# A two-block fp32 network on one core: the rows of silu(c) made by TensorE, the first loads in one queue and another order, and the input-norm generator of layer 1 queued later

## The chip, the cores and the metric

The kernel runs on one core of one Trainium2 chip. The metric is the device time of one execution in microseconds. It is given as the median of three runs. The engines are named as the profile names them: PE is TensorE (its weight loads are PEld), DVE is VectorE, ACT is ScalarE, POOL is GpSimd, and SP is SyncE, which here only issues DMAs.

## The reference

Two blocks follow each other. The first has two layers over 1024 tokens of x and 256 tokens of context, 1024 wide. The second has one layer and a gated feed-forward part. What the change touches lies in the first block:

```python
def hybrid_layer(x, xc, c_act, cc_act, w_mod, b_mod, ...):
    shift, scale, gate = jnp.split(c_act @ w_mod + b_mod, 3, axis=-1)
    h = x * (1 + scale[:, None]) + shift[:, None]
    rk, rv, nk, nv, rq, rg, nq, ng, ch, cb, ccg, cz = split_cols(h @ w_in, PROJ_SPLITS)
    ...
    y = jnp.concatenate([y_conv, y_ret, y_na], axis=-1) @ w_out
    x_new = layer_norm(DEEPNORM_ALPHA * x + gate[:, None] * y, ln_g, ln_b)

def first_block(...):
    c_act = jax.nn.silu(c)
    cc_act = jax.nn.silu(c_ctx)
    for l in range(DEPTH):
        x, xc = hybrid_layer(x, xc, c_act, cc_act, ...)
```

`y_ret` is a retention over 6 heads, forward and backward, and `y_na` is an attention over a window of 8 x 16 neighbours and the context, with 6 heads.

## The kernel before

Every fp32 product is split: an operand is a high part that TensorE takes at its fast fp32 form and a low part, and three matmuls (high x high, high x low, low x high) are summed. So a weight block is loaded raw (`wr`), ACT makes its high part (`wh`) and POOL its low part (`wl = wr - wh`); three raw buffers and three pairs of high and low rotate. The split of hidden states is the same work on ACT and DVE (`xh`, `xl` for x, `ch`, `cl` for the context).

The order of the work is set by a planner, the class Mixer. It keeps a modelled time `vt` that advances with each TensorE product. Generators for side work (retention pairs, attention pairs, modulation blocks and so on) are queued with `mix.add`. Each main product earns credit (`ratio` times its own time), and while there is credit the first generator that is due is stepped, so that side work stands between main products. `R_RET` is that ratio in the retention part. A generator that yields a number is due again that many nanoseconds later. `mix.drain()` steps all that is left, moving `vt` on to each generator's due time. TensorE's queue has the order in which products are emitted. On the other engines instructions are ordered by the modelled start time that they had (plus `late`, 5000 ns for the generators with X_MOD); on the chip each queue then runs strictly in order, SP's queue of DMA issues too.

The start. `setup` loads c as a column (`cvec`) and, by two broadcast DMAs, as rows (`crow`, each 128 x 1024). `hidden0_load(k)` loads for one of 8 blocks of 128 features a column block of the scale weights transposed (`wmT`), a block of the shift weights (`wm`) and x and context transposed (`xr`, `xc`). `hidden0` makes block k of the modulated hidden state: `mod_block` reduces wmT times each row of `crow` on DVE (into `mjk`), which gives the scale; eight small products `cact, wm` on TensorE give the shift; ACT applies both; `split` makes the high and low parts. `ready_k` runs `STEPS` blocks ahead of the first main product that needs block k. The first main products (`wh`, `wl` against `xh`, `xl`, `ch`, `cl`) are the values of the retention heads.

The end of a layer. The attention pairs n0 to n2 run beside main products. Then come gate blocks, `mix.drain()`, and the output projection, which reads `yr` (the layer's y back from DRAM, split to `yhl`) against `w_out`, one weight block for twelve matmuls. Its result is normalised. `x1_gen` belongs to layer 1: layer 0 left its norm without gain and bias in DRAM (`xn`), and this generator loads each of 8 token tiles, multiplies by the gain and adds the bias on POOL (tiles `x`, 128 x 1024, against `lnbc`), and stores them as `x1`, which the end of layer 1 reads. It is a loop of these lines:

```python
for t in range(8):
    x = self.S("x1")
    self.nc.sync.dma_start(out=x, in_=self.xn[sl])
    yield
    self.tt(x, x, gb[0], ALU.mult, self.nc.gpsimd)
    self.tt(x, x, gb[1], ALU.add, self.nc.gpsimd)
    self.nc.sync.dma_start(out=self.x1[0][sl], in_=x)
    self.free(x)
    yield 6000
```

In profiles, line L344 is the helper of every matmul, L349 that of every transpose, and L251 records each operation of the other engines.

Of the kernel before, what the change touches and what calls it, by code (L numbers as in the profile page):

```python
# [12 lines left out]
AF = mybir.ActivationFunctionType  # L13
ALU = mybir.AluOpType
AX = mybir.AxisListType

NX = 1024
NC = 256
NT = NX + NC
# [7 lines left out]
class Mixer:  # L27
# [92 lines left out]
    late = 0.0  # L120
# [362 lines left out]
class Layers(Base):  # L483
    X_RET = (1500, 1500)
    AHEAD = 3
    STEPS = 2
# [3 lines left out]
    def setup(self):  # L490
        nc, io = self.nc, self.io
        self.cvec = self.const("cvec", [128, 16])
        nc.sync.dma_start(out=self.cvec, in_=io["c_cols"])
        self.bmod = self.const("bmod", [128, 48])
        nc.sync.dma_start(out=self.bmod, in_=io["b_mod"])
        self.crow = [self.S("crow") for _ in range(2)]
        for j in range(2):
            nc.scalar.dma_start(out=self.crow[j], in_=io["c_rows"][j:j + 1, :].to_broadcast([128, 1024]))
        self.mjk = self.S("mjk")
        self.h0 = {}  # L500
        for k in range(self.AHEAD):
            self.hidden0_load(k)
        self.ident = self.const("ident", [128, 128])
        nc.sync.dma_start(out=self.ident, in_=io["c_ident"])
        self.ones = self.const("ones", [128, 128])
        nc.vector.memset(self.ones, 1.0)
        self.mhalf = self.const("mhalf", [128, 16])
        nc.gpsimd.memset(self.mhalf, -0.5)
        self.lncol = self.const("lncol", [128, 32])
        nc.sync.dma_start(out=self.lncol, in_=io["ln_col"])  # L510
        self.convw = self.const("convw", [128, 16])
        nc.sync.dma_start(out=self.convw, in_=io["conv"])
        self.iota = self.const("iota", [128, 4])
        nc.sync.dma_start(out=self.iota, in_=io["c_iota"])

        self.cact = self.const("cact", [128, 8, 2])
        t = self.small("cs", [128, 16])
        self.act(t, self.cvec, AF.Tanh, scale=0.5)
        self.stt(t, t, 1.0, self.cvec, ALU.add, ALU.mult)
        for j in range(2):  # L520
            self.ts(self.cact[:, :, j], t[:, 8 * j:8 * j + 8], 0.5, None, ALU.mult)
        for c in self.crow:
            t = self.S("crt")
            self.act(t, c, AF.Tanh, scale=0.5)
            self.stt(c, t, 1.0, c, ALU.add, ALU.mult)
            self.free(t)

        self.ts(self.bmod[:, 8:16], self.bmod[:, 8:16], 1.0, None, ALU.add)

        self.mod = [self.const(f"mod{l}", [128, 3, 8, 2]) for l in range(2)]  # L530

    def mod_block(self, l, b, w, nctx=2):

        acc = self.small("macc", [128, 2])
# [3 lines left out]
        part, kk = divmod(b, 8)  # L538
        self.ts(self.mod[l][:, part, kk, 0:nctx], acc[:, 0:nctx], 0.5, self.bmod[:, 24 * l + b:24 * l + b + 1], ALU.mult, ALU.add)
# [17 lines left out]
    def hidden0_load(self, k):  # L557
        if k < 8:
            io, nc = self.io, self.nc
# [3 lines left out]
            nc.scalar.dma_start(out=t, in_=io["xT"][k * 128:(k + 1) * 128, 0:NX])  # L563
            nc.scalar.dma_start(out=c, in_=io["xT"][k * 128:(k + 1) * 128, NX:NT])
# [35 lines left out]
    def ret_consts(self, l):  # L600
# [3 lines left out]
        nc.sync.dma_start(out=E, in_=io["c_E"])  # L604
        nc.sync.dma_start(out=x, in_=io["ret_decay"][l:l + 1, :].to_broadcast([128, 12]))
# [478 lines left out]
    R_RET = 10.0  # L1084
# [16 lines left out]
    def layer(self, l, hT, need_ctx, ready=None, ready_k=None):  # L1101
# [24 lines left out]
        for s in self.ORDER1[l].split():  # L1126
# [11 lines left out]
            else:  # L1138
                if p == 0 and l == 1:
                    mix.add(self.x1_gen(), True, peak=3, late=self.X_MOD)  # L1140
# [474 lines left out]
    def block1(self, stop=None):  # L1615
        nc, io, mix = self.nc, self.io, self.mix
        self.done_o, self.ready = set(), set()
        self.w_init()
        for l in range(2):
            self.layer_weights(l)  # L1620
# [963 lines left out]
def host_layout(inputs):  # L2584
# [15 lines left out]
    a["c_rows"] = np.concatenate([f("c"), f("c_ctx")[None]], 0)  # L2600
# [109 lines left out]
```

## Time and profile before

| | before |
|---|---|
| runs | 2966.71, 2963.77, 2957.46 us |
| median | 2963.77 us |
| profiled execution | 2959.18 us |
| its span | 2957.4 us |
| mean granted TensorE clock | 0.957 |
| busy: PE, DVE, ACT, POOL | 92%, 67%, 40%, 33% |

The profiled execution is one of the kernel, taken apart from the three runs; its span goes from the first to the last instruction, and the rest of its time lies around that. Busy shares are of the span. A granted clock of 1.00 is the full rate.

### The profile page before, as it was taken

What the parts mean: (1) busy time and instruction counts of PE and PEld (TensorE: products, weight loads), DVE (VectorE), ACT (ScalarE), POOL (GpSimd) and SP (SyncE); (2) the same over time, 40 slices, a digit from 0 to 9 for tenths busy, and PEclk for the clock granted to TensorE, in tenths of its full rate; (3) what the DMA queues carried; (4) which work ended last, traced back from release to release, by engine and by line L of the source; (5) the groups of instructions that cost most, each with busy time, mean ns of one, the idle gap of its engine ahead of it and who ended that gap; (6) DMA issues with size and microseconds to landing.
All of it is one profiled execution on the core that took longest, in us unless ns stands there. A gap on an engine that the chain in (4) does not pass through costs nothing. (4 is left out here: it accounts for less than half of the span.)

```text
span 2957.4 us, 41337 instructions
## 1 busy us (share of the span) xinstructions
PE 2722.3 (92%) x14572; PEld 2342.2 (79%) x14572; DVE 1985.9 (67%) x4011; ACT 1190.1 (40%) x2715; POOL 971.4 (33%) x836
## 2 busy tenths in 40 slices
PE   6989999999989989979999977899998999999998
PEld 6977888898788878768787766787876788887886
DVE  6866675774642557667554697868844588786687
ACT  5212254563332225445443332456653333333443
POOL 4443512213433441451563332111135244443001
PEclk9988999999999999989999979999999999999999
DMA  7533302216333221433543543222343222223874
GB/s 254 180 103 124 93 32 78 82 65 202 127 108 100 65 70 34 154 119 131 169 135 108 170 139 123 99 72 85 109 158 125 96 107 107 107 96 122 305 252 168
DMA packets 173071, 367.87 MB, mean 124 GB/s; under 512 B 30048, under 2 KB 57984, under 8 KB 172864
## 3 DMA queue, kind: packets, MB, share of 16 engines
q1 hardware_dynamic: 160064, 343.07, 34.3%
q10 hardware_dynamic: 10016, 13.12, 1.8%
q0 software_dynamic: 2784, 9.05, 1.0%
q8 instruction: 115, 1.88, 0.3%
q14 instruction: 92, 0.75, 0.1%
HBM read 279.35 MB, written 79.51 MB: 121 GB/s over the span
## 5 line engine op out<-in xcount | busy, mean ns | idle before, releaser
L251 POOL TENSOR_TENSOR wl<-wr,wh 128x512 fp32r<-128x512 f32 (+2 forms) x344 | 452.1, 1318 | 1151.0 <-ACT wh L251 1046.9
L344 PE MATMUL pb<-xl,wh 128*128 128x512 f32 x1456 | 580.2, 399 | 0.0
L344 PE MATMUL pb<-xh,wl 128*128 128x512 f32 x1456 | 579.5, 398 | 0.6 <-POOL wl L251 0.6
L344 PE MATMUL pb<-xh,wh 128*128 128x512 f32 x1456 | 579.1, 398 | 0.0
L251 ACT ACTIVATE wh<-wr 128x512 fp32r<-128x512 f32 (+2 forms) x344 | 202.7, 591 | 401.7 <-PE pb L344 314.4
L344 PEld LDWEIGHTS pb<-xh,wl 128*128 128x128 f32 x1456 | 277.6, 191 | 56.5 <-POOL wl L251 1.0
L344 PEld LDWEIGHTS pb<-xl,wh 128*128 128x128 f32 x1456 | 277.8, 191 | 54.1 <-issue 0.2
L344 PEld LDWEIGHTS pb<-xh,wh 128*128 128x128 f32 x1456 | 277.7, 191 | 53.0 <-issue 0.3
L344 PE MATMUL pb<-wh,yhl 128*128 128x512 f32 x832 | 264.0, 396 | 7.0 <-DVE xl L251 4.4
L344 PE MATMUL pb<-T,wh 128*128 128x512 f32 x640 | 196.9, 389 | 0.0
L344 PEld LDWEIGHTS pb<-wh,yhl 128*128 128x128 f32 x832 | 158.4, 191 | 41.3 <-issue 6.0
L251 POOL TENSOR_TENSOR wl<-ws,wh 128x512 fp32r<-128x512 f32 x100 | 135.0, 1350 | 155.4 <-ACT wh L251 154.0
L344 PE MATMUL pb<-wl,yhl 128*128 128x512 f32 x416 | 164.8, 396 | 5.1 <-POOL wl L251 5.1
L344 PE MATMUL pb<-whi,yhl 128*128 128x512 f32 x528 | 164.0, 392 | 4.5 <-DVE yhl L251 4.5
L251 ACT ACTIVATE pt<-pb 128x512 fp32r<-128x512 f32 (+3 forms) x230 | 114.0, 528 | 132.4 <-PE pb L349 115.5
L251 DVE TENSOR_TENSOR pt<-pb,pt 128x512 fp32r<-128x512 f32 (+3 forms) x230 | 130.0, 595 | 51.5 <-ACT pt L251 50.3
L344 PEld LDWEIGHTS pb<-T,wh 128*128 128x128 f32 x640 | 120.1, 188 | 25.0
L251 DVE TENSOR_TENSOR yhl<-yr,yhl 128x512 fp32r<-128x512 f32 (+2 forms) x133 | 97.6, 760 | 61.4 <-ACT yhl L251 52.4
L251 ACT ACTIVATE wh<-ws 128x512 fp32r<-128x512 f32 x100 | 63.2, 632 | 172.7 <-PE pb L344 172.7
L344 PE MATMUL pb<-wl,xh 128*128 128x384 f32 (+1 forms) x384 | 125.9, 328 | 5.9 <-POOL wl L251 5.9
L344 PE MATMUL pb<-wh,xl 128*128 128x384 f32 (+1 forms) x384 | 126.0, 328 | 3.4 <-ACT wh L251 1.3
L344 PE MATMUL pb<-wh,xh 128*128 128x384 f32 (+1 forms) x384 | 125.4, 327 | 0.0
(434 smaller groups left out, 6009.5 us busy)
## 6 DMA issues: line engine op xcount, KB each, us to landing
wr<-in_w_in_dram SPq DMA_DIRECT2D x152, 256.0 KB, 2.7
ws<-in_w_down_dram SPq DMA_DIRECT2D x110, 256.0 KB, 5.6
wr<-in_w_out_dram SPq DMA_DIRECT2D x96, 256.0 KB, 2.9
yr<-ffn SPq DMA_DIRECT2D x33, 512.0 KB, 5.8
wm<-in_w_modT_dram SPq DMA_DIRECT2D x32, 512.0 KB, 4.8
wr<-in_w_v_dram SPq DMA_DIRECT2D x64, 192.0 KB, 2.4
ws<-in_w_gate_dram SPq DMA_DIRECT2D x22, 512.0 KB, 5.3
ws<-in_w_up_dram SPq DMA_DIRECT2D x22, 512.0 KB, 6.1
```

What stands on the lines that cost most here:

```text
L251: return fn(*a, **kw)
L344: self.mix.product(c / 2.4, out, (lhsT, rhs), lambda: self.nc.tensor.matmul(out, lhsT, rhs, start=start, stop=stop))
```

## The change

Setup makes the rows of silu(c) from the column form: for each of the two vectors DVE writes eight 128 x 128 blocks, the identity times one column of silu(c) (`crt`), TensorE multiplies them with a matrix of ones in two products of 512 columns, and ACT copies the results to `crow`. The two broadcast loads, two tanh and two products on whole rows go; the factor 0.5 is now in `cact`, so `mod_block` drops it. `ident` and `bmod` are loaded in ACT's queue. The transposed x and context move from ACT's queue to SP's, behind the weights of their block, and the first three value weights stand between the loads of block 0 and block 1. `STEPS` is 1. The load of layer 0's retention decay gets a copy in front that reads the last modulation scale, so that it can't be issued before that is there. `R_RET` is 2. `x1_gen` is no longer started at gate block 0 of layer 1 but queued at gate block 2.

```diff
@@ setup
         nc.sync.dma_start(out=self.cvec, in_=io["c_cols"])
+        self.ident = self.const("ident", [128, 128])
+        nc.scalar.dma_start(out=self.ident, in_=io["c_ident"])
         self.bmod = self.const("bmod", [128, 48])
-        nc.sync.dma_start(out=self.bmod, in_=io["b_mod"])
+        nc.scalar.dma_start(out=self.bmod, in_=io["b_mod"])
+        self.h0 = {}
+        self.hidden0_load(0)
+        self.w_init()
+        self.layer_weights(0)
+        self.w_load(self.NRAW)
+        self.hidden0_load(1)
...
+        self.act(t, self.cvec, AF.Tanh, scale=0.5)
+        self.stt(t, t, 1.0, self.cvec, ALU.add, ALU.mult)
+        for j in range(2):
+            self.ts(self.cact[:, :, j], t[:, 8 * j:8 * j + 8], 0.5, None, ALU.mult)
         self.crow = [self.S("crow") for _ in range(2)]
         for j in range(2):
-            nc.scalar.dma_start(out=self.crow[j], in_=io["c_rows"][j:j + 1, :].to_broadcast([128, 1024]))
+            t = self.S("crt", (128, 8, 128))
+            for k in range(8):
+                self.ts(t[:, k], self.ident, self.cact[:, k, j:j + 1], None, ALU.mult)
+            for i in range(2):
+                ps = self.bank()
+                self.mm(ps, self.ones, t[:, 4 * i:4 * i + 4])
+                self.act(self.crow[j][:, 512 * i:512 * i + 512], ps)
+            self.free(t)
...
-        for k in range(self.AHEAD):
+        for k in range(2, self.AHEAD):
             self.hidden0_load(k)
...
-        for c in self.crow:
-            t = self.S("crt")
-            self.act(t, c, AF.Tanh, scale=0.5)
-            self.stt(c, t, 1.0, c, ALU.add, ALU.mult)
-            self.free(t)
@@ class Layers
-    STEPS = 2
+    STEPS = 1
...
-    R_RET = 10.0
+    R_RET = 2.0
@@ mod_block
-        self.ts(self.mod[l][:, part, kk, 0:nctx], acc[:, 0:nctx], 0.5, self.bmod[:, 24 * l + b:24 * l + b + 1], ALU.mult, ALU.add)
+        self.ts(self.mod[l][:, part, kk, 0:nctx], acc[:, 0:nctx], self.bmod[:, 24 * l + b:24 * l + b + 1], None, ALU.add)
@@ hidden0_load
-            nc.scalar.dma_start(out=t, in_=io["xT"][k * 128:(k + 1) * 128, 0:NX])
-            nc.scalar.dma_start(out=c, in_=io["xT"][k * 128:(k + 1) * 128, NX:NT])
+            nc.sync.dma_start(out=c, in_=io["xT"][k * 128:(k + 1) * 128, NX:NT])
+            nc.sync.dma_start(out=t, in_=io["xT"][k * 128:(k + 1) * 128, 0:NX])
@@ ret_consts
+        if l == 0:
+            nc.vector.tensor_copy(x[:, 0:1], self.mod[0][:, 1, 7, 0:1])
         nc.sync.dma_start(out=x, in_=io["ret_decay"][l:l + 1, :].to_broadcast([128, 12]))
@@ the pairs of layer l
-                if p == 0 and l == 1:
-                    mix.add(self.x1_gen(), True, peak=3, late=self.X_MOD)
+                if p == 2 and l == 1:
+                    mix.add(self.x1_gen(), peak=3, late=self.X_MOD)
@@ block1
-        self.w_init()
-        for l in range(2):
-            self.layer_weights(l)
+        self.layer_weights(1)
```

What the planner makes of it is seen in three queues. First POOL in layer 1's output projection. Names `wl` are low parts of weights, and `x` the tiles of x1_gen. Before (`wl_13735` is the first weight of the projection, and all of x1_gen stands earlier):

```order
L251 TENSOR_TENSOR wl_13729<-wr_13361,wh_13728 128x512
L251 TENSOR_TENSOR wl_13735<-wr_13367,wh_13734 128x512
L251 TENSOR_TENSOR wl_13893<-wr_13726,wh_13892 128x512
L251 TENSOR_TENSOR wl_13917<-wr_13732,wh_13916 128x512
L251 TENSOR_TENSOR wl_13939<-wr_13890,wh_13938 128x512
L251 TENSOR_TENSOR wl_13961<-wr_13914,wh_13960 128x512
```

Now (`wl_13728` is the first weight; each tile x has two rows, of which the first is shown, except for the last):

```order
L251 TENSOR_TENSOR wl_13728<-wr_13346,wh_13727 128x512
...
L251 TENSOR_TENSOR x_2763_13652<-x_2763_13652,lnbc_13575 128x1024
...
L251 TENSOR_TENSOR wl_13916<-wr_13719,wh_13915 128x512
L251 TENSOR_TENSOR wl_13940<-wr_13725,wh_13939 128x512
L251 TENSOR_TENSOR x_2794_13763<-x_2794_13763,lnbc_13575 128x1024
...
L251 TENSOR_TENSOR x_2797_13801<-x_2797_13801,lnbc_13575 128x1024
...
L251 TENSOR_TENSOR x_2800_13816<-x_2800_13816,lnbc_13576 128x1024
L251 TENSOR_TENSOR wl_13962<-wr_13913,wh_13961 128x512
L251 TENSOR_TENSOR wl_13984<-wr_13937,wh_13983 128x512
```

Two tiles (four rows) now stand between the first and the second weight of the projection, and six tiles (twelve rows) between the third and the fourth.

Second, SP's queue at the same place, where `x_0_56_192` is the store of a tile x and `xn_194` its source. Now:

```order
L251 DMA x_0_56_192<-x_2797_13801 128x1024
L251 DMA x_2799_13811<-xn_194 128x1024
L251 DMA x_2800_13816<-xn_194 128x1024
L251 DMA x_0_56_192<-x_2798_13806 128x1024
...
L251 DMA x_0_56_192<-x_2799_13811 128x1024
L251 DMA yr_13899<-yT_5_51_187 128x512
L251 DMA x_0_56_192<-x_2800_13816 128x1024
L251 DMA yr_13931<-yT_6_52_188 128x512
L251 DMA wr_13937<-in_w_out_dram 128x512
L251 DMA yr_13955<-yT_7_53_189 128x512
```

The raw load of the fifth weight (`wr_13937`, which `wl_13984` above reads) and the last two `yr` now stand behind the store of the last tile x; before, no transfer of x1_gen stood among them.

Third, DVE at the start. Before:

```order
L251 TENSOR_SCALAR cact<-cs_120 128x8 x2
L251 SCALAR_TENSOR_TENSOR crow_78<-crt_125,crow_78 128x1024
L251 SCALAR_TENSOR_TENSOR crow_79<-crt_128,crow_79 128x1024
L251 ISA mjk_82,macc_192<-wmT_83,crow_78 128x1024
...
L251 ISA mjk_82,macc_256<-wmT_99,crow_78 128x1024
...
L251 TENSOR_TENSOR cl_187<-xc_86,ch_186 128x256
```

Now:

```order
L251 TENSOR_SCALAR cact<-cs_105 128x8 x2
L251 TENSOR_SCALAR crt_112<-ident,cact 128x128 x8
L251 TENSOR_SCALAR crt_127<-ident,cact 128x128 x8
L251 ISA mjk_143,macc_220<-wmT_80,crow_110 128x1024
...
L251 ISA mjk_143,macc_309<-wmT_144,crow_110 128x1024
...
L251 TENSOR_TENSOR cl_215<-xc_83,ch_214 128x256
```

The sixteen blocks take the place of the two products on rows, and block 0's low part `cl` stands, as before, behind the reduction of block 2's `wmT`.

## Rows read from the trace of the kernel before

**Rows 1.** The page of the profile: busy time and share of each engine.
```profile
PE 2722.3 (92%) x14572; PEld 2342.2 (79%) x14572; DVE 1985.9 (67%) x4011; ACT 1190.1 (40%) x2715; POOL 971.4 (33%) x836
```

**Rows 2.** Stretches: start:end, length, then busy us per engine, granted clock, DMA share, GB/s.
```profile
0.00:50.00 50.00, 29.05 (x153) 28.09 (x154) 30.77 (x51) 22.64 (x42) 15.73 (x15) 1.00 0.91 319
...
1235.00:1298.00 63.00, 38.77 (x214) 34.61 (x213) 45.94 (x104) 27.15 (x79) 35.68 (x23) 0.78 0.36 124
...
1400.00:1435.00 35.00, 35.00 (x156) 28.99 (x155) 12.80 (x16) 12.91 (x22) 17.39 (x13) 1.00 0.58 181
```

**Rows 3.** Timeline of TensorE, start: start us, us, instruction, [idle before, what ended it].
```profile
10.91 1.41 PE L344 MATMUL pb<-cact,wm 128*128 128x2 f32 x6 [10.91 <-DMA wm<-in_w_mod_dram]
...
30.68 0.69 PE L344 MATMUL pb<-wh,cl 128*128 128x384 f32 x1 [9.22 <-DVE cl L251]
...
56.64 0.66 PE L344 MATMUL pb<-wh,cl 128*128 128x384 f32 x1 [4.25 <-DVE mod L251]
...
61.30 1.84 PE L344 MATMUL pb<-cact,wm 128*128 128x2 f32 x16
```

**Rows 4.** Timeline of VectorE, start of the kernel.
```profile
17.61 2.36 DVE L251 SCALAR_TENSOR_TENSOR crow<-crt,crow 128x1024 f32<-128x1024 f32 x2 [11.54 <-ACT crt L251]
19.89 1.22 DVE L251 CUSTOM_DVE_ANT_0 mjk<-wmT,crow 128x1024 f32<-128x1024 f32 x1
...
56.08 0.41 DVE L251 TENSOR_TENSOR cl<-xc,ch 128x256 fp32r<-128x256 f32 x1
```

**Rows 5.** DMA view of 44 to 46 us, SP's queue: packets, MB, share of 16 engines.
```profile
q1 hardware_dynamic: 225, 0.79, 101.3%
```

**Rows 6.** Groups of TensorE by form: busy us, mean ns; a product with ones.
```profile
L344 PE MATMUL pb<-dg,ones 128*128 128x128 f32 x48 | 6.5, 298 | 1.0 <-DVE dg L251 1.0
```

**Rows 7.** Waits of TensorE, 235 to 275 us: total us, times, longest us.
```profile
PE pb L344 <- DVE sd L251: 1.2, 1, 1.2
```

**Rows 8.** Waits of TensorE, 1236 to 1298 us.
```profile
PE pb L349 <- DVE sl L251: 19.5, 5, 5.9
PE pb L344 <- DVE pt L251: 4.5, 2, 2.3
```

**Rows 9.** Waits of TensorE, 540 to 575 us (the same stretch of layer 0).
```profile
PE pb L349 <- DVE sl L251: 3.2, 3, 1.9
PE pb L344 <- DVE pt L251: 2.0, 2, 1.7
```

**Rows 10.** Timeline of VectorE and of POOL from 1258 us.
```profile
1258.34 0.34 DVE L251 TENSOR_SCALAR sl<-sl,rsm 128x256 f32<-128x256 f32 x1
1258.60 2.42 DVE L251 TENSOR_SCALAR sc<-sc,rsm 128x256 f32<-128x256 f32 x1
1260.95 2.56 DVE L251 TENSOR_SCALAR sl<-sl,rsm 128x384 f32<-128x384 f32 x1
...
1258.35 4.95 POOL L251 TENSOR_TENSOR x<-x,lnbc 128x1024 f32<-128x1024 f32 x2 [4.61 <-DMA yT<-go]
```

**Rows 11.** Instructions on the tiles x, 1210 to 1320 us: min/median/max ns, first and last start.
```profile
L251 POOL TENSOR_TENSOR x<-x,lnbc x16: 2338/2384/2532, 1217.4 to 1313.8; 128x1024 f32<-128x1024 f32 x16
```

**Rows 12.** Timeline of POOL, from 1397 us: the low parts of weights.
```profile
1397.93 1.29 POOL L251 TENSOR_TENSOR wl<-wr,wh 128x512 fp32r<-128x512 f32 x1 [18.79 <-ACT wh L251]
1400.64 1.49 POOL L251 TENSOR_TENSOR wl<-wr,wh 128x512 fp32r<-128x512 f32 x1 [1.42 <-ACT wh L251]
1403.59 1.44 POOL L251 TENSOR_TENSOR wl<-wr,wh 128x512 fp32r<-128x512 f32 x1 [1.46 <-ACT wh L251]
```

**Rows 13.** Timeline of TensorE, layer 1's output projection.
```profile
1399.90 0.39 PE L344 MATMUL pb<-wh,yhl 128*128 128x512 f32 x1
...
1408.29 0.39 PE L344 MATMUL pb<-wl,yhl 128*128 128x512 f32 x1
```

**Rows 14.** DMA issues of the page: count, KB each, median us from issue to landing.
```profile
wr<-in_w_out_dram SPq DMA_DIRECT2D x96, 256.0 KB, 2.9
```

More of the change, by code (lines that the diff above doesn't have):

```diff
@@ L493, in setup @@
         nc.sync.dma_start(out=self.cvec, in_=io["c_cols"])
+        self.ident = self.const("ident", [128, 128])
+        nc.scalar.dma_start(out=self.ident, in_=io["c_ident"])
         self.bmod = self.const("bmod", [128, 48])
-        nc.sync.dma_start(out=self.bmod, in_=io["b_mod"])
+        nc.scalar.dma_start(out=self.bmod, in_=io["b_mod"])
[5 more added lines that the diff above has]
+        self.hidden0_load(1)
+        self.ones = self.const("ones", [128, 128])
+        nc.vector.memset(self.ones, 1.0)
+        self.cact = self.const("cact", [128, 8, 2])
+        t = self.small("cs", [128, 16])
+        self.act(t, self.cvec, AF.Tanh, scale=0.5)
+        self.stt(t, t, 1.0, self.cvec, ALU.add, ALU.mult)
+        for j in range(2):
+            self.ts(self.cact[:, :, j], t[:, 8 * j:8 * j + 8], 0.5, None, ALU.mult)
         self.crow = [self.S("crow") for _ in range(2)]
         for j in range(2):
-            nc.scalar.dma_start(out=self.crow[j], in_=io["c_rows"][j:j + 1, :].to_broadcast([128, 1024]))
+            t = self.S("crt", (128, 8, 128))
[6 more added lines that the diff above has]
+            self.free(t)
+        self.ts(self.bmod[:, 8:16], self.bmod[:, 8:16], 1.0, None, ALU.add)
         self.mjk = self.S("mjk")
-        self.h0 = {}
-        for k in range(self.AHEAD):
+        for k in range(2, self.AHEAD):
             self.hidden0_load(k)
[L503 to L506, printed above, removed]
         self.mhalf = self.const("mhalf", [128, 16])
@@ L514, in setup @@
         nc.sync.dma_start(out=self.iota, in_=io["c_iota"])
[L516 to L521, printed above, removed]
-        for c in self.crow:
-            t = self.S("crt")
-            self.act(t, c, AF.Tanh, scale=0.5)
-            self.stt(c, t, 1.0, c, ALU.add, ALU.mult)
-            self.free(t)
-        self.ts(self.bmod[:, 8:16], self.bmod[:, 8:16], 1.0, None, ALU.add)
         self.mod = [self.const(f"mod{l}", [128, 3, 8, 2]) for l in range(2)]
@@ L2599, in host_layout @@
     a["w_modT"] = np.ascontiguousarray(wm.transpose(0, 2, 1)).reshape(2, 24, 128, 1024)
-    a["c_rows"] = np.concatenate([f("c"), f("c_ctx")[None]], 0)
     w = f("w_in")
```

## The prediction

> **What bounds the kernel now.** I read the busy shares first: TensorE works 92% of the span [rows 1], and nothing in the change removes work from it, so a gain can only come out of TensorE's idle time or its slow stretches, and a loss can only be new idle time. Then I read stretches of 50 us, and looked for those with idle time next to the places that the diff touches. Three matter [rows 2]: the first 50 us (29.05 us busy), the drain of layer 1's attention at 1235 to 1298 us (38.77 us busy of 63, granted clock 0.78), and the output projection of layer 1 from 1400 us, where TensorE has no idle time at all at a clock of 1.00. The timeline says what ends each idle time.
>
> **The start.** TensorE's first product waits 10.91 us for `wm`, the first main product stands at 30.68 after a wait of 9.22 us for `cl`, and the first main product of block 4 at 56.64 after 4.25 us [rows 3]. Behind the second wait stands DVE: it could not begin the reductions (`mjk`) before `crow` was made, at 17.61 to 19.89 us [rows 4], and from there to 61 us it shows one idle time, of some 2 us. So DVE's late start is the price of the broadcast rows, and the loads are close behind it.
>
> What the change does here. Two broadcast loads (512 KB written each), two tanh and two DVE products of 1.2 us each go [rows 4]. Sixteen DVE writes of 128x128 come: a 128x256 TENSOR_SCALAR takes 0.34 us [rows 10], so they cost 2.7 to 5.4 us together. Four TensorE products of 512 columns in plain fp32 come: nearest are the 128-column products with ones at 0.298 us [rows 6], so from 0.3 to 1.2 us each; both run before any block can be consumed. I take `crow` as ready at about 10.5 us (constants in at 4 to 5 us, 3.5 us of DVE, then TensorE and four ACT copies behind three `wh`): DVE starts its reductions some 9 us earlier. The rest is not that much earlier, because loads now set the pace. SP's queue alone moved 0.79 MB in 2 us [rows 5], some 395 GB/s, so one queue does not cost rate; but 50 us at 319 GB/s [rows 2] are 16 MB, and about 15 MB of it is still to come before block 7 is in. At 360 to 395 GB/s, with two pauses where a dozen small loads stand in the eight-deep queue, block 7's `wmT` lands at about 45 us. DVE has `cl` of block 4 behind that reduction, so block 4's main products begin at 46 to 48 us instead of 56.64, and one step `cact, wm` (half of `STEPS`) comes later than before: the 16 matmul records of one took 1.84 us [rows 3]. Gain 56.6 - 47 - 1.8, about 8 us. Bounds: 12 (loads at full rate) and 0 (the loads land as late as before). The tied decay load makes `rax` on DVE wait some 2.5 us for a DMA, with `cl` and `xl` of blocks 6 and 7 behind it; TensorE has the main products of blocks 4 and 5 meanwhile, about 9 us, so I cost it at nothing; without that cover it is 2.5 us. The factor 0.5 and the copy are free on DVE.
>
> **Credit 2 in retention.** The packed first retention products keep their place; only behind them do main products stand between them. There TensorE waits only 1.2 us by semaphores [rows 7]. Gain 1 us, bounds -1 and 5.
>
> **x1_gen moves.** It takes 16 POOL rows of 2.384 us [rows 11] out of 1217 to 1316 us and puts them at 1380 to 1431 us.
>
> What it gives back: at 1236 to 1298 us TensorE waits 19.5 us for `sl` and 4.5 us for `pt` [rows 8]. The same drain in layer 0, with no x1_gen, has waits of 3.2 and 2.0 us [rows 9]. The timeline shows why: two DVE operations that take 0.34 us alone take 2.42 and 2.56 us, just while POOL has two `x` rows from 1258.35 to 1263.30 [rows 10]. In the new order the drain has the products of layer 0's, plus one more softmax round behind it, for which I leave 2.5 us. 24.0 - 5.2 - 2.5 is 16.3 us; the higher clock there adds some 2 us. Gain 18 us, bounds 10 (only the waits during an `x` row go) and 26 (all of it). The Trainium skill (SBUF — State Buffer, section "SBUF: two separate sides") says that DVE and GpSimd share a port pair as an exclusive lock, held for the whole instruction. The two long rows end right after the two `x` rows do, as that says.
>
> What it costs: layer 1's output projection uses one weight in about 2.72 us, from 1399.90 on [rows 13], and POOL makes each `wl` just ahead, the third at 1400.64, the fourth at 1403.59 [rows 12]. Now twelve `x` rows stand between those two. The third ends at 1402.1; twelve rows of 2.384 us are 28.6 us; the fourth `wl` (1.44 us) ends at 1432.1. TensorE wants it at 1408.29 [rows 13]: a wait of 23.8 us. Nothing else can run, since TensorE's queue is in order. Next, the raw load of the fifth weight stands on SP behind the store of the last tile, at 1430.7; with 2.9 us to land [rows 14], a `wh` (0.6 us, my estimate: half of a `wl`) and a `wl` of 1.3 it is ready at 1435.5 to 1436, when TensorE would want it at 1434.6: another 1.2 us. After such waits the granted clock is lower for a while, as in the stretch with 0.78 [rows 2]: 2 us, an estimate. The four `x` rows ahead meet the tail of the last attention pair on DVE: 1 us. Cost 28 us, bounds 22 (twelve rows half begun when the projection starts) and 40.
>
> Elsewhere the planner's side work shifts by a few units, in the recurrent part of the second block most; the operations stay, and no row gives a sign: 0, bounds 5 either way, about layer 0's drain in [rows 9].
>
> **Sum.** -8 - 1 - 18 + 28 = +1 us on the profiled execution's 2959.2, so 2960. The median of the runs stands 4.6 us above that execution; the forecast in its terms is 2963.8 + 1, **2964 us**. About 0.3% (9 us) is what a measurement of this kernel can tell from no change.
>
> **Rivals.**
> *Faster (0.32), about 2949 us.* The start and the drain give their upper halves: TensorE's whole 24 us in the drain go, as only DVE's collisions made them, and the loads run at SP's full rate. -11 - 2 - 24 + 24 is -13 to -15. For it: rows 8 against 9 are a factor of four to five. Against it: the order of the projection leaves the cost no room to shrink below 22.
> *Slower by a new chain in the projection (0.16), about 2977 us.* Loads and stores of `x` alternate on SP: the load of a tile is issued only after the store of the one two before it. If a landing takes more than the 4.8 us that POOL needs for a tile, POOL waits between tiles, as it did before (16 rows stretched from 1217.4 to 1313.8 [rows 11]). Four late loads by 3 us each add 12 us. It decides from a landing of about 5 us on; rows 14 show 2.9 us for half the bytes, which speaks against it.
> *Slower by DVE holding POOL (0.05), about 2974 us.* DVE is busy 12.80 us in 1400 to 1435 [rows 2]; if its operations hold up the `x` rows as those held DVE, up to that, say 10 us, is added. That would be the lock of the Trainium skill (SBUF — State Buffer, section "SBUF: two separate sides") in the other direction. The trace speaks against it: the longest `x` row is 2532 ns, the shortest 2338 [rows 11], with DVE busy beside them.
> *Slower because the start doesn't gain (0.09), about 2973 us.* The change would then not do what it says: the small loads in the one queue cost what the broadcasts cost, and block 7 lands at 52 us again. +1 + 8 is +9, at the edge of what can be told.
>
> **How the numbers follow.** Forecast 0.38. Faster by over 0.3% is the first rival, 0.32; slower by over 0.3% the other three, 0.30. The forecast's own range is 2955 to 2972. The range that should hold 8 in 10 takes in the first rival to -20 (start 12, drain 26, cost 24, the rest 6 less in part) and the chain to +19: 2944 to 2983.
>
> **What would show it.** Right: the first main product at 18 to 21 us and block 4's at 46 to 48; waits for `sl` and `pt` in layer 1's drain of 6 to 12 us in all; `sc` rows of 0.34 us there; one TensorE wait of 22 to 28 us for `wl` in layer 1's output projection, with POOL full of `x` rows in front. Wrong: no such wait, so that POOL had time for `x` earlier; a wait for `sl` as long as before; block 7's load at 50 us or later; or a new wait over 5 us in the second block.

## The result, and the profile after

| | before | changed |
|---|---|---|
| median of 4 runs | 2963.88 us (2957.46 to 2966.71) | 2988.83 us (2986.7 to 2993.21) |
| ratio, 95% interval | | 1.0089 [1.0069, 1.0109] |
| profiled execution (its span) | 2959.18 us (2957.4) | 2988.15 us (2986.4) |

The change makes the kernel 25 us slower. The forecast was 2964 us, and the range ended at 2983: the result lies outside it. TensorE is busy 11 us longer than in [rows 1], and the span is 29 us longer, so most of the loss is new idle time. Page of the changed kernel, busy time by engine:

```profile
PE 2733.1 (92%) x14580; PEld 2343.3 (78%) x14580; DVE 1986.4 (67%) x4026; ACT 1188.9 (40%) x2717; POOL 966.4 (32%) x836
```

To find where it went I took the products of activations with weights one after the other in each trace and set the start of the n-th against the start of the n-th before. The first, for one, starts at 30.68 us before [rows 3] and at 21.42 us now: -9.3. The growth of that offset from mark to mark is each stage's part. A positive number is time lost; all are us from one profile each, and experiments (described below) stand beside the change:

| stage (time before at its end) | changed | e1 | e2 | e3 | e4 | e7 | e8 | e10 | e11 |
|---|---|---|---|---|---|---|---|---|---|
| start (186.5) | +4.9 | +6.4 | -1.2 | +7.5 | +3.2 | +5.8 | +2.7 | +2.1 | -1.7 |
| layer 0, retention (383.5) | -3.6 | -3.8 | -4.2 | -0.9 | -4.1 | -4.7 | -3.5 | -2.8 | -2.1 |
| to layer 1's retention (858.0) | +2.7 | +2.9 | +3.3 | +2.1 | +3.5 | +2.6 | +0.3 | +1.5 | +1.1 |
| layer 1, retention (1110.4) | -5.6 | -5.6 | -5.8 | +0.7 | -5.8 | +19.7 | -4.6 | -5.4 | -5.8 |
| layer 1, to the drain (1220.9) | +0.1 | 0.0 | 0.0 | -0.1 | 0.0 | 0.0 | +0.1 | +29.6 | +0.1 |
| drain of the attention (1306.2) | -20.5 | -2.1 | -20.5 | -20.6 | -2.3 | -28.1 | -20.6 | -28.2 | -6.4 |
| to the projection (1394.5) | -0.8 | -0.7 | -0.8 | +6.1 | -0.6 | +2.4 | -0.2 | -0.2 | -0.4 |
| output projection (1421.7) | +36.8 | 0.0 | +36.8 | +33.8 | +0.4 | 0.0 | +22.6 | 0.0 | 0.0 |
| to the recurrent part (1852.1) | -3.6 | -3.7 | -1.2 | -3.3 | -0.8 | -2.7 | -2.1 | -0.6 | -0.1 |
| recurrent part, block 2 (2193.4) | +15.8 | -1.2 | +16.8 | +15.7 | -0.6 | -1.5 | +18.2 | +3.5 | -0.7 |
| the rest (2945.8) | +2.8 | +0.5 | +5.6 | +2.9 | +3.2 | +0.6 | +0.4 | +5.8 | +0.5 |
| sum | +29.0 | -7.3 | +28.8 | +43.9 | -3.9 | -5.9 | +13.3 | +5.3 | -15.5 |

Three stages carry the result: the drain gives back 20.5 us, the projection costs 36.8, and the recurrent part of the second block costs 15.8.

**The drain** did what was forecast. Windows of the changed kernel (columns as in [rows 2]), its waits of TensorE from 1236 to 1298 us (as in [rows 8]) and its instructions on `sc` there (as in [rows 11]):

```profile
1235.00:1298.00 63.00, 56.27 (x312) 49.18 (x311) 42.49 (x118) 32.64 (x90) 13.94 (x18) 0.89 0.20 67
```

```profile
PE pb L349 <- DVE sl L251: 6.0, 5, 3.3
PE pb L344 <- DVE pt L251: 0.6, 1, 0.6
```

```profile
L251 DVE TENSOR_SCALAR sc<-sc,rsm x10: 341/345/349, 1245.0 to 1268.3; 128x256 f32<-128x256 f32 x10
```

The waits fall from 24.0 us [rows 8] to 6.6, which is 17.4 of the 20.5 us; TensorE is busy 56.27 of 63 us instead of 38.77 [rows 2], and no `sc` row is longer than 349 ns, where one took 2.42 us before [rows 10].

**The projection** has two long waits where before there was none. Waits of TensorE from 1375 to 1430 us:

```profile
PE pb L344 <- ACT wh L251: 22.4, 1, 22.4
PE pb L344 <- DVE yhl L251: 8.4, 1, 8.4
PE pb L344 <- POOL wl L251: 0.6, 1, 0.6
```

The releasers are named ACT and DVE, and `x1_gen` stands behind both: with `x1_gen` alone put back (e1, below) neither wait is left. The timeline of the changed kernel, here of five queues one after the other (TensorE, POOL, ACT, DVE, then SP's DMA issues):

```profile
1385.67 0.77 PE L344 MATMUL pb<-wh,yhl 128*128 128x512 f32 x1 [8.39 <-DVE yhl L251]
1418.76 0.80 PE L344 MATMUL pb<-wh,yhl 128*128 128x512 f32 x1 [22.41 <-ACT wh L251]
...
1382.64 16.24 POOL L251 TENSOR_TENSOR x<-x,lnbc 128x1024 f32<-128x1024 f32 x6 [3.52 <-DMA x<-xn]
1399.51 14.18 POOL L251 TENSOR_TENSOR x<-x,lnbc 128x1024 f32<-128x1024 f32 x6 [0.63 <-DMA x<-xn]
...
1378.16 2.69 ACT L251 ACTIVATE yhl<-yr 128x512 fp32r<-128x512 f32 x5
1412.73 0.63 ACT L251 ACTIVATE yhl<-yr 128x512 fp32r<-128x512 f32 x1 [31.88 <-DMA yr<-yT]
1417.56 0.63 ACT L251 ACTIVATE yhl<-yr 128x512 fp32r<-128x512 f32 x1 [4.20 <-DMA yr<-yT]
1418.10 0.61 ACT L251 ACTIVATE wh<-wr 128x512 fp32r<-128x512 f32 x1
...
1380.09 0.69 DVE L251 SCALAR_TENSOR_TENSOR go<-th,go 128x512 f32<-128x512 f32 x1 [13.99 <-DMA go<-oscr]
1382.75 13.94 DVE L251 TENSOR_TENSOR yhl<-yr,yhl 128x512 fp32r<-128x512 f32 x5
...
1413.72 0.32 SPq L251 DMA_DIRECT2D x<-x  x1
1414.14 0.38 SPq L251 DMA_DIRECT2D yr<-yT  x1
```

Read it from the second wait backwards. TensorE goes on at 1418.76, when the high part of the fourth weight (`wh`, 1418.10) is there. ACT makes that behind the high part of an activation block (1417.56), which waits for its load `yr`. That load stands on SP behind the store of a tile `x` and is issued at 1414.14; the store is issued at 1413.72, right when POOL's twelfth `x` row ends (1399.51 + 14.18 = 1413.69).

The first wait has a chain of its own. TensorE ran out of products at 1377.3 us, and it waited for the first of DVE's five splits `yhl`, which began at 1382.75 only: ahead of it on DVE stood the operations `go`, which had waited 13.99 us for their load. SP issued that load at 1375.48, behind a small store (`oscr`) that took 8.0 us to land, against 3.0 us before. SP had just waited 4.0 us for a POOL row before it could store a tile `x`, and then issued that store, the next tile's load and the loads behind them in one burst; the DMA engines were busy for 1.00 to 1.02 of the time from 1365 to 1376 us. That makes some 5.5 of the 8.4 us. The split itself makes most of the rest: 2.78 us instead of 0.69 where one stands alone, beside the `x` rows on POOL. All five take 13.94 us beside six rows, which also take longer, 2.7 us each instead of 2.384 [rows 11], but TensorE waited for the first one alone.

**The recurrent part** of block 2 has longer waits for DVE, from 1890 to 2200 us of the changed kernel:

```profile
PE pb L344 <- DVE pt L251: 14.6, 5, 6.9
PE pb L349 <- DVE dsl L251: 6.7, 9, 2.5
```

The same stage (1877 to 2172 us) of the kernel before, a place that the prediction had not looked at:

```profile
PE pb L344 <- DVE pt L251: 6.2, 4, 3.9
...
PE pb L349 <- DVE dsl L251: 2.4, 2, 1.7
```

These two explain 12.7 of the 15.8 us. The longest, 6.9 us, is the "new wait over 5 us in the second block" that the prediction named as a sign of being wrong.

**The start.** The first main product came at 21.42 us, just past the 18 to 21 us forecast, but block 4's at 57.38, later than the 56.64 of before. Timeline of TensorE:

```profile
6.95 5.94 PE L344 MATMUL pb<-crt,ones 128*128 128x512 f32 x8 [6.95 <-DVE crt L251]
21.42 0.69 PE L344 MATMUL pb<-wh,cl 128*128 128x384 f32 x1 [5.07 <-DVE cl L251]
37.19 0.69 PE L344 MATMUL pb<-wh,cl 128*128 128x384 f32 x1 [4.92 <-ACT xh L251]
...
44.60 3.41 PE L344 MATMUL pb<-cact,wm 128*128 128x2 f32 x16
...
52.66 1.84 PE L344 MATMUL pb<-cact,wm 128*128 128x2 f32 x16
57.38 0.69 PE L344 MATMUL pb<-wh,cl 128*128 128x384 f32 x1 [2.88 <-DVE cl L251]
```

And windows of ten us of the same kernel, then of the kernel before:

```profile
20.00:30.00 10.00, 8.56 (x44) 8.38 (x45) 8.19 (x16) 3.60 (x6) 3.42 (x2) 0.74 0.84 289
30.00:40.00 10.00, 4.56 (x26) 3.96 (x24) 6.15 (x10) 7.49 (x15) 4.77 (x4) 0.77 1.01 391
40.00:50.00 10.00, 8.45 (x32) 8.45 (x33) 7.81 (x12) 2.45 (x4) 2.22 (x2) 0.50 0.79 309
50.00:60.00 10.00, 7.12 (x34) 7.03 (x33) 3.03 (x5) 5.28 (x11) 2.17 (x2) 0.67 0.07 20
```

```profile
40.00:50.00 10.00, 9.74 (x67) 9.42 (x67) 9.93 (x14) 7.80 (x16) 6.35 (x5) 1.00 1.02 400
```

The work began earlier, but it came in pieces with waits between. Block 1's main products began 10.8 us earlier than before (27.70 against 38.50), block 2's 5.7 us earlier (37.19 against 42.91), block 3's at the same time (47.87 against 47.86). The first half went into the wait of 4.92 us for `xh`. The second went into one of 2.07 us for `xl` and into products at the lower clock: the granted clock was 0.50 from 40 to 50 us (the lower level, 1.2 GHz), where before it was 1.00, with 32 products in ten us instead of 67, and block 4's step `cact, wm` (at 44.60) took 3.41 us, against 1.84 [rows 3]. By this reading some 7 of the 10.8 us went into waits and some 4 into the clock.

Block 4 then waited neither for loads (0.07 of the DMA engines' time after 50 us) nor for the reduction that stands ahead of `cl` on DVE, which was through at 47.9 us. Timeline of ACT, then of DVE, of the changed kernel:

```profile
54.54 0.26 ACT L251 ACTIVATE mod<-pb,bmod 128x2 f32<-128x2 f32 x1 [1.11 <-PE pb L344]
56.47 0.70 ACT L251 ACTIVATE ch<-xc 128x256 fp32r<-128x256 f32 x2
...
56.90 0.76 DVE L251 TENSOR_TENSOR cl<-xc,ch 128x256 fp32r<-128x256 f32 x2 [8.98 <-ACT ch L251]
```

DVE stood idle for 8.98 us until ACT had made `ch` of block 4. In ACT's queue that stands behind the modulation of block 5 (`mod`, 54.54), which waits for block 5's step on TensorE, at 52.66; and this step stands in order behind block 3's products, which ran at the lower clock.

### The profile page after: what moved, and what is told of

It is laid out like the page before. It is cut to its first block, busy times and chain, and to the rows that moved or that the text cites. A ratio compares the mean times of both kernels' runs of the same rounds, so it can differ in the third digit from the quotient of the medians.

```text
span 2986.4 us, 41337 instructions
## 1 busy us (share of the span) xinstructions
PE 2733.1 (92%) x14580; PEld 2343.3 (78%) x14580; DVE 1986.4 (67%) x4026; ACT 1188.9 (40%) x2717; POOL 966.4 (32%) x836
## 5 line engine op out<-in xcount | busy, mean ns | idle before, releaser
L344 PE MATMUL pb<-wh,yhl 128*128 128x512 f32 x832 | 270.2, 404 | 39.0 <-ACT wh L251 22.6
L251 DVE TENSOR_TENSOR yhl<-yr,yhl 128x512 fp32r<-128x512 f32 (+2 forms) x133 | 106.9, 832 | 81.8 <-ACT yhl L251 81.6
```

Of the source, the lines that this page charges most:

```text
L251: return fn(*a, **kw)
L344: self.mix.product(c / 2.4, out, (lhsT, rhs), lambda: self.nc.tensor.matmul(out, lhsT, rhs, start=start, stop=stop))
```

## The experiments

The theory after the result: `x1_gen`'s new place is the whole loss, the start gives nothing, and credit 2 gives more than was thought. The rivals: the recurrent part's loss comes from the credit or the start; `STEPS` at 1 spoils a gain of the start; any other place for `x1_gen` is as dear. Each was timed beside the kernel before on the same chip, and ratios are to that; its median was 2957.48 us beside e1 to e4, 2959.47 beside e5 to e8 and 2960.73 beside e9 to e12.

### e1: x1_gen put back

```diff
-                if p == 2 and l == 1:
-                    mix.add(self.x1_gen(), peak=3, late=self.X_MOD)
+                if p == 0 and l == 1:
+                    mix.add(self.x1_gen(), True, peak=3, late=self.X_MOD)
```

> The changed kernel with x1_gen started at gate block 0 of layer 1 again; everything else as changed. Theory: the move of x1_gen alone is worth +27 us (drain of layer 1 -20.5, output projection +37, the second block's recurrent stage +13 to +16, a few us of small gains behind the projection), so this kernel is 2960 to 2964 us; TensorE's waits for wh and yhl in layer 1's projection are gone and its waits in the recurrent stage are those of the kernel before, since the order of products there is again the one of before. Rival: the loss in the recurrent stage comes from the credit or the start; then it stays, and the kernel is 2973 to 2978 us.

Measured 2957.12 us against 2957.48, ratio 0.9995 [0.998, 1.0009]. That is 3 us below the range expected, and no different from the kernel before. The drain's gain (but for 2.1 us), the projection's loss and the recurrent part's loss all go (column e1). So all three belong to the move of `x1_gen`, and the rest of the change together is not measurable in the total. Waits of e1's recurrent part:

```profile
PE pb L344 <- DVE pt L251: 6.2, 4, 4.0
...
PE pb L349 <- DVE dsl L251: 2.4, 2, 1.7
```

They are those of the kernel before. Nothing of `x1_gen` runs in that stage. What differs is the order that the planner writes: in e1, e4, e7 and e11 TensorE's products of the second block stand in the order of before, in the changed kernel, e2, e3 and e8 in another (it differs from 1877 to 2165 us of the kernel before), and in e10 in a third. The four kernels of the other order lose 15.7 to 18.2 us there, the four of the old one nothing, e10 3.5 us; in e8 no row of `x1_gen` is on POOL at all. In the code the drain of the side work at the layer's end steps through what `x1_gen` still holds and pushes the planner's clock on before the next stage is laid out; this is read in the code, not measured.

### e2, e4 and e12: STEPS

e2 is the changed kernel with `STEPS` at 2, e4 is e1 with the same, and e12 is the kernel before with `STEPS` at 1.

```diff
-    STEPS = 1
+    STEPS = 2
```

> The changed kernel with STEPS 2. Theory: the start lost 5 us instead of gaining 8 because with STEPS 1 the shift products of a block stand behind the main products of the block two before it in TensorE's queue, so that each block's chain (shift, ACT, split) starts only when they end; with STEPS 2 block 4's main products start at 44 to 50 us instead of 57.4, and the kernel is 2972 to 2981 us. Rival: the loads in one queue with a dozen small ones set the pace; then block 4's main products stay at 55 us or later and the time is that of the changed kernel, 2985 to 2992 us.

> The changed kernel with x1_gen started at gate block 0 again and STEPS 2: rows of silu(c) by TensorE, the new loads and credit 2 remain. Theory: the parts add, so 2947 to 2954 us, faster than the kernel before by 10 to 17 us. Rival: the loads set the pace of the start; then 2958 to 2964 us, no different from before.

> The kernel before with STEPS 1 alone. Theory: STEPS 1 by itself costs 4 to 6 us at the start, since each block's shift products stand behind the main products of the block two before: 2962 to 2966 us against 2959 for before. Rival: STEPS costs only with the new loads; then no difference, 2956 to 2961 us.

Measured: e2 2990.38 against 2957.48, 1.0108 [1.0091, 1.0125]; e4 2954.22 against 2957.48, 0.9988 [0.9975, 1.0002]; e12 2963.51 against 2960.73, 1.0006 [0.9994, 1.0018]. No case of `STEPS` can be told from no change by itself. e2's profile is 6.1 us better than the changed kernel's at the start, and next to none of it is left at the end; block 4's main products begin at 55.1 us there, not at 44 to 50, so the rival's numbers came. e4 is 3 us faster than the kernel before, not the 10 to 17 us of its theory. The start differs between profiles as well: with `STEPS` at 2 and otherwise nearly the same start seven profiles (e2, e4 and e7 to e11) have offsets of -1.7 to +5.8 us at 186.5 us (mean 1.8), with 1 three have 4.9, 6.4 and 7.5; e12, with the loads of before, has 1.3. So `STEPS` may cost some 4 us of the start, no more, and the timings do not show it.

### e3: credit 10 again

```diff
-    R_RET = 2.0
+    R_RET = 10.0
```

> The changed kernel with R_RET 10. Theory: credit 2 gains 6 to 7 us (3.6 in layer 0's retention, 5.7 in layer 1's, less some 2.7 between), so this kernel is 2993 to 2998 us. Rival: the gains in the two retention parts come from elsewhere (layer 0's start running late, x1_gen away); then the time is within 3 us of the changed kernel.

Measured 3001.6 us against 2957.48, ratio 1.0137 [1.0112, 1.0162]. Against the changed kernel's 1.0089 that is 0.0048, 14 us; with both intervals it can be anything from some 5 to 24 us, so it is not told apart from the 6 to 7 expected. In the stages e3 loses 2.7 us to the changed kernel in layer 0's retention, 6.3 in layer 1's and 6.9 ahead of the projection, and gains 3.0 in it. The 6.9 can't be put down to the credit: the kernel before, with credit 10 too, has nothing there, and e9, with credit 2, loses 5.0 there against it. Windows of layer 1's retention, of before, changed and e3:

```profile
858.00:1112.00 254.00, 243.82 (x1431) 211.28 (x1429) 112.48 (x253) 63.93 (x145) 102.60 (x87) 0.96 0.29 82
```

```profile
858.00:1111.00 253.00, 244.26 (x1456) 211.36 (x1455) 114.85 (x251) 64.20 (x146) 103.05 (x89) 0.99 0.30 83
```

```profile
866.00:1120.00 254.00, 243.76 (x1428) 211.43 (x1427) 112.14 (x252) 63.31 (x144) 101.52 (x87) 0.96 0.29 82
```

Busy and idle time of these windows are nearly the same in all three, but the changed kernel has the granted clock at 0.99 instead of 0.96, and it gets through 25 more products than before and 28 more than e3. Taken from the stage's first product to its last, TensorE is busy 238.1 us and idle 8.7 in the changed kernel, 242.9 and 10.2 in e3: 4.8 us are faster products, 1.5 fewer waits. In layer 0's retention the clock is the same (0.91 in both), and the gain is idle time (14.4 us against 16.7).

### e5, e6 and e9: the start in parts

e5 is the kernel before with the rows of silu(c) from TensorE alone, e6 the kernel before with the new queue and order and the tied decay load alone. e9 is e4 with six later small loads tied to the last modulation scale too, as the decay load is.

```diff
@@ e5
+        self.ident = self.const("ident", [128, 128])
+        nc.sync.dma_start(out=self.ident, in_=io["c_ident"])
...
-            nc.scalar.dma_start(out=self.crow[j], in_=io["c_rows"][j:j + 1, :].to_broadcast([128, 1024]))
...
+                self.ts(t[:, k], self.ident, self.cact[:, k, j:j + 1], None, ALU.mult)
...
+                self.mm(ps, self.ones, t[:, 4 * i:4 * i + 4])
@@ e6
-            nc.scalar.dma_start(out=t, in_=io["xT"][k * 128:(k + 1) * 128, 0:NX])
-            nc.scalar.dma_start(out=c, in_=io["xT"][k * 128:(k + 1) * 128, NX:NT])
+            nc.sync.dma_start(out=c, in_=io["xT"][k * 128:(k + 1) * 128, NX:NT])
+            nc.sync.dma_start(out=t, in_=io["xT"][k * 128:(k + 1) * 128, 0:NX])
...
+            nc.vector.tensor_copy(x[:, 0:1], self.mod[0][:, 1, 7, 0:1])
@@ e9
+        tie = lambda t: nc.vector.tensor_copy(t[:, 0:1], self.mod[0][:, 1, 7, 0:1])
...
+        tie(self.al)
```

> The kernel before with one part of the change: the rows of silu(c) come from TensorE (ident loaded right behind c on SP, the broadcast loads gone, the factor 0.5 dropped); loads and queues otherwise as before. Theory: the broadcasts were the price of the start, as the prediction had it, so reductions on DVE start at 10 to 13 us instead of 19.9, block 4's main products at 49 to 53 us instead of 56.6, and the kernel is 4 to 8 us faster than before, 2950 to 2954 us. Rival: the loads behind set the pace and nothing comes of it, 2955 to 2960 us.

> The kernel before with the other part of the start: one queue, the new order of loads and the tied decay load, but rows of c by broadcast loads as before, and STEPS 2, credit 10 and x1_gen at gate block 0 as before. Theory: the new order puts a dozen small loads and three weights ahead of block 2's loads, whose wm all blocks' ACT work stands behind, so that the start loses 2 to 6 us: 2959 to 2964 us. Rival: one queue in the order of use gains by itself: 2948 to 2955 us.

> The kernel of e4 (change with x1_gen back and STEPS 2) with the six small loads of the second block (onorm_col, conv2, msk2, c_bd, tini, al) tied to the last scale of modulation, as the change ties the decay load. Theory: small loads in the eight-deep queue and ACT's gea, which waits for one of them, hold the start; without them blocks 4 to 7 come 2 to 4 us earlier, so main products are dense 2 to 4 us earlier than in e4, and the kernel is 2948 to 2953 us. Rival: what paces the start is the serial work per block on ACT, DVE and TensorE; then it is as e4, 2952 to 2957 us.

Measured: e5 2963.0 against 2959.47, 1.0006 [0.9991, 1.0021]; e6 2958.97 against 2959.47, 0.9995 [0.9982, 1.0009]; e9 2957.01 against 2960.73, 0.9987 [0.9975, 0.9998], as e4. None of the parts gains, nor does e6 lose the 2 to 6 us of its theory, and the loads that e9 takes out of the way were not what held the start. Why e5 gains nothing is seen on ACT. Timeline of ACT before:

```profile
27.71 0.52 ACT L251 ACTIVATE wh<-wr 128x384 fp32r<-128x384 f32 x1 [4.01 <-DMA wr<-in_w_v_dram]
28.14 0.58 ACT L251 ACTIVATE xc<-xc,mod 128x256 f32<-128x256 f32 x1
```

In ACT's queue block 0's `xc` stood behind the high parts of value weights, of which the last ahead of it landed at 27.7 us. Its scale was there at 23.7 us; the first main product of 30.68 us [rows 3] waited for a weight's load, and not for `crow`. Timeline of ACT in e5:

```profile
21.82 0.52 ACT L251 ACTIVATE wh<-wr 128x384 fp32r<-128x384 f32 x1 [6.89 <-DMA wr<-in_w_v_dram]
...
23.13 0.59 ACT L251 ACTIVATE crow<-pb 128x512 f32<-128x512 f32 x1
...
28.87 0.60 ACT L251 ACTIVATE xc<-xc,mod 128x256 f32<-128x256 f32 x1 [4.08 <-DVE mod L251]
```

Without the broadcasts these weights are through some 3 us earlier, and `xc` is as late as ever, now by its scale from DVE. For e5 did not do what it was made for: DVE's reductions were to start at 10 to 13 us and started at 24.33, later than the 19.89 of before [rows 4]. The last copy of the rows (`crow`, 23.13) stands in ACT's queue behind the high part of a weight that landed at 21.8, and DVE had `rax` in front, which waited for the load of the decay until 22.93. So e5 shows that this edit alone gains nothing, not that early rows alone would not; in the changed kernel the reductions did start early.

### e8: x1_gen's rows on DVE, in the new place

The changed kernel with `STEPS` at 2, and x1_gen's two row operations on DVE instead of GpSimd.

```diff
-            self.tt(x, x, gb[0], ALU.mult, self.nc.gpsimd)
-            self.tt(x, x, gb[1], ALU.add, self.nc.gpsimd)
+            self.tt(x, x, gb[0], ALU.mult)
+            self.tt(x, x, gb[1], ALU.add)
```

> The changed kernel with STEPS 2, x1_gen where the change has it, but its two operations on DVE instead of POOL. Theory: POOL's twelve rows between the third and the fourth weight made most of the new wait in the projection; with POOL free, the wait for wh and yhl (31 us together) shrinks to 5 to 15 us, and the kernel is 2968 to 2978 us. Rival: SP's order (the fifth weight and the last yr behind the stores) makes the wait by itself; then 20 us or more of it stay, and the kernel is 2980 to 2990 us.

Measured 2972.72 us against 2959.47, ratio 1.0045 [1.0031, 1.0058]. The projection's loss falls from 36.8 to 22.6 us. The time is in the theory's range, but the wait did not shrink to the 5 to 15 us expected: it is one of 20.6 us for `yhl`, since the `x` rows now stand ahead of the splits on DVE. Timeline of DVE in e8:

```profile
1378.57 10.54 DVE L251 TENSOR_TENSOR x<-x,lnbc 128x1024 f32<-128x1024 f32 x9
1391.60 2.48 DVE L251 TENSOR_TENSOR x<-x,lnbc 128x1024 f32<-128x1024 f32 x2 [2.49 <-DMA x<-xn]
1394.00 3.09 DVE L251 TENSOR_TENSOR yhl<-yr,yhl 128x512 fp32r<-128x512 f32 x5
```

With POOL free of `x`, the five splits take 3.09 us instead of 13.94. The recurrent part's loss stays (18.2), as the order of the second block is the new one.

### e7 and e10: x1_gen earlier, in two other places

e7 starts it before layer 1's first retention block, e10 at its second convolution block; both with `STEPS` at 2 and without the start at gate block 2.

```diff
@@ e7
+            if l == 1 and s == "r0":
+                mix.add(self.x1_gen(), True, peak=3, late=self.X_MOD)
...
-                if p == 2 and l == 1:
-                    mix.add(self.x1_gen(), peak=3, late=self.X_MOD)
@@ e10
+            if l == 1 and s == "c1":
+                mix.add(self.x1_gen(), True, peak=3, late=self.X_MOD)
```

> The changed kernel with STEPS 2 and x1_gen started at the first retention pair of layer 1, far from the drain and the projection. Theory: it keeps the drain's gain of some 20 us, loses nothing in the projection and nothing in the recurrent stage (whose order of products is that of the kernel before again): 2934 to 2946 us, faster than all kernels so far. Rival: POOL's rows hold up DVE in retention as they did in the drain; then retention of layer 1 is 10 us or more longer, and the kernel 2948 to 2960 us.

> The changed kernel with STEPS 2 and x1_gen started at conv block 1 of layer 1, between the first two attention pairs. Theory: there main products are dense, so POOL's rows cost less than in retention (e7 lost 20 us there) and the drain keeps its gain; the recurrent stage gets a third order of products, whose loss is unknown, between 0 and 16 us: 2935 to 2955 us, most likely 2943. Rival: wherever the rows stand beside attention they hold up DVE's softmax by 20 us: 2955 to 2975 us.

Measured: e7 2952.44 against 2959.47, ratio 0.9969 [0.9957, 0.9982]; e10 2962.16 against 2960.73, 1.0 [0.9985, 1.0016]. Both times are those of the rivals. Both free the drain fully (-28), and both pay for it where the rows land: e7 25 us in the retention (+19.7, where the other kernels with credit 2 have some -5.6), e10 29.6 us beside the attention. Waits of TensorE in e7, 860 to 1136 us:

```profile
PE pb L349 <- DVE O L251: 8.8, 2, 6.8
PE pb L344 <- POOL wl L251: 5.7, 2, 5.0
PE pb L344 <- DVE St L251: 4.6, 1, 4.6
```

In e10, 1110 to 1290 us:

```profile
PE pb L349 <- DVE sl L251: 13.5, 6, 7.7
PE pb L344 <- ACT wh L251: 5.4, 1, 5.4
```

So sixteen rows on POOL are dear in each place tried: some 26 us in the old one (the drain's -2.1 of e1 against -28), 25 and 29.6; the changed kernel's place costs 36.8, of which 22.6 stay in e8 with the rows off POOL. e7 gains 0.3% in all: the drain's 28 us outweigh the 25, the projection loses nothing, and the recurrent part keeps the old order.

### e11: x1_gen in the old place, on DVE

e4 with the edit of e8.

> The kernel of e4 (x1_gen at gate block 0) with the two operations of x1_gen on DVE. Theory: the drain lost its 20 us because POOL's rows of 2.4 us held up DVE's short operations; on DVE they are 16 operations of some 1.2 us, 19 us of DVE work in the drain, where DVE is the bound, so the drain gains little: TensorE's waits for sl and pt there stay at 12 to 24 us, and the kernel is 2946 to 2956 us. Rival: only the hold of the port mattered and the drain's waits fall to 6 to 10 us: 2935 to 2945 us.

Measured 2944.15 us against 2960.73, ratio 0.9946 [0.9931, 0.9961]. **This beats both kernels.** The time is the rival's, the waits are the theory's. Of the 15.5 us in its profile 8.4 are there before the drain (credit 2, and a good start), and the drain gives 6.4. Against e4, from which it differs by this edit alone, it is some 12 us faster in the timings; in the profiles the drain makes 4.1 us of 11.6, while 4.9 lie at the start and 2.6 in the rest, which the edit does not touch. So only a third of what the edit gave is located. Waits of TensorE from 1220 to 1290 us, and the instructions on the tiles `x`:

```profile
PE pb L349 <- DVE sl L251: 18.0, 3, 7.6
```

```profile
L251 DVE TENSOR_TENSOR x<-x,lnbc x16: 1203/1220/1226, 1208.2 to 1281.7; 128x1024 f32<-128x1024 f32 x16
```

A row takes 1.22 us on DVE instead of 2.38 on POOL. The drain still waits 18.0 us for `sl`, now, as I read it, because sixteen `x` rows (19.5 us) stand in DVE's own queue; but they are done sooner, and nothing behind the drain gets worse.

## Why the prediction was wrong

**The drain (-18): right.** -20.5 in the profile, by the mechanism named: without `x` rows on POOL DVE's short operations stay short, and 17.4 us of waits go, where 16.3 were forecast.

**The projection (+28): right in its mechanism, mis-sized; measured +36.8.** The forecast wait of 23.8 us for the fourth weight came, as 22.4 us, but that they are so near is in part luck. By POOL's rows alone the low part would have been there at about 1415.0 (1413.69 and a `wl` of 1.27), a wait of some 18 us. The chain through SP and ACT made it 4 us longer: the weight's high part stood on ACT behind two activation blocks, whose loads stand on SP behind the stores of `x`. I had a rival chain through SP at 0.16, by another link than this one. Left out were the 8.4 us for `yhl`: I costed twelve rows in POOL's queue, and not SP's burst of transfers, which made DVE's `go` late (5.5 us), nor DVE's splits beside the rows (2.1 us on the first). The first six rows themselves took 2.7 us instead of 2.384, and POOL sat 3.52 us before them for a load. The granted clock of 0.72 from 1375 to 1435 us costs more than the 2 us that I set; the row:

```profile
1375.00:1435.00 60.00, 28.65 (x104) 22.31 (x103) 19.96 (x14) 9.74 (x18) 41.28 (x21) 0.72 0.58 197
```

After 31.4 us of waits, about 5 of the 36.8 are left for it. The rival that DVE's work would hold up POOL (0.05) came in small only: POOL's six rows stretched by 2 us in all, and DVE's five splits by some 11. The Trainium skill (SBUF — State Buffer, section "SBUF: two separate sides") says that a DVE operation with two inputs from SBUF takes the shared port pair against a GpSimd operation that reads SBUF; the 13.94 us beside POOL's rows and the 3.09 without them agree with that.

**"Elsewhere 0, bounds 5": this step failed; measured +15.8 in the recurrent part of the second block.** "The operations stay, and no row gives a sign" was the argument, and it took an order of the planner's for free. The new order took the waits for `pt` and `dsl` from 8.6 to 21.3 us. I had given no rival to it. With the projection's 9 us and the start's 13 it puts the result outside the range, though the drain and credit 2 gave 11 us more than forecast.

**The start (-8): failed; +4.9 in the profile, and no timing shows a gain of any part.** The step was "DVE's late start is the price of the broadcast rows, and the loads are close behind it". DVE did begin at 11.48 us, close to the 10.5 forecast, and block 7's rows were in before 46.7 us, as forecast. But "DVE has `cl` of block 4 behind that reduction, so block 4's main products begin at 46 to 48 us" left out ACT: `cl` waited 8.98 us for `ch`, which stood in ACT's queue behind block 5's modulation, and that on a step of TensorE. Already before, the first main product had waited for a weight on ACT, so the late rows alone were not the price. Waits of 4.92 and 2.07 us and products at half the clock took the head start back by block 3.

**Credit 2 (-1): right sign, mis-sized.** 9 us in the two retentions and 14 us in the timings, the latter with a wide interval. I counted one stretch's waits (1.2 us [rows 7]); in layer 1 4.8 of the 6.3 us are the clock, in layer 0 the gain is waits. Why the clock is higher there is open.

Put together: with the start at +4.9, the two retentions at -9.2, the drain at -20.5, the projection at +36.8 and the recurrent part at +15.8, the sum is 27.8 of the 29.0 us.

**Open.** Why the new order of the recurrent part is worse, beyond the two waits, was not tried: no experiment forced one order with the other place of `x1_gen`. Most of what e11 gained over e4 is not located. The start is not settled finer than the spread of the profiles, some 4 us either way.

## What to carry to other kernels

Side work taken out of one stage is paid where it lands: before moving it, list at the new place every in-order queue that it enters (here POOL, SP, and through SP's loads ACT and DVE), and who stands behind it there. In a kernel whose order a planner writes, moving one item can reorder a stage some 600 us later, so compare the order of the whole program, and treat a reordered stage as an unknown with a price. An earlier first product is worth nothing by itself if the next blocks wait on another engine's queue and their products come in pieces at half the clock.

## What the runs showed of the hardware

- DVE and POOL side by side: five 128x512 differences of two SBUF inputs took 13.94 us on DVE beside six 128x1024 POOL rows, and 3.09 us with none; the POOL rows took 2.7 us instead of 2.36 (the six behind them in the same run).
- The same 128x1024 operation on two tiles (`x` times or plus `lnbc`) takes 1.22 us on DVE (e11) and 2.38 us on POOL (before).
- A TensorE product in plain fp32 of 512 columns shows as two records; four of them at the start of the kernel took 5.94 us, 1.5 us each, above the 1.2 that I had set as the upper bound. The first records start 0.86 us apart and the last three 0.43, so at the faster rate a product takes 0.86 us, inside the bounds.
- The same products of layer 1's retention ran at a granted clock of 0.99 or 0.96, with only the credit of their order changed (changed kernel and e3): 246.8 us against 253.1.
